# Hybrid attention and DeltaNet step: a modulation slab moved, column groups tied, late half norms, and weight splits taken off GpSimd

## Chip, cores and metric

The kernel runs on one core of a Trainium2 chip in one launch. The metric is device time in microseconds (us) of that core, as the median of several executions. One further execution was profiled, and the rows below come from it. Engine names are those of the profile: PE (TensorE matmul), PEld (its weight load), DVE (VectorE), ACT (ScalarE), POOL (GpSimd) and SP (SyncE, which issues most DMAs).

## What is computed (the reference, cut)

One step of a two layer model on 128 context tokens and 512 latent tokens, with width 1024. Layer 0 mixes tokens by attention, layer 1 by a gated delta rule; each layer has a squared ReLU MLP of width 4096. Each layer draws six modulation vectors from a conditioning vector, by one 1024 x 6144 matrix per layer.

```python
def modulation(cond, w_mod, b_mod):
    m = jax.nn.silu(cond) @ w_mod + b_mod
    return jnp.split(m[..., None, :], N_MOD, axis=-1)

def trunk_layer(x, mods, gain1, gain2, w1, w2, mixer):
    shift1, scale1, gate1, shift2, scale2, gate2 = mods
    mix, aux = mixer(rms_norm(x, gain1) * (1 + scale1) + shift1)
    x = x + gate1 * mix
    h = rms_norm(x, gain2) * (1 + scale2) + shift2
    x = x + gate2 * (jnp.square(jax.nn.relu(h @ w1)) @ w2)
    return x, aux
```

The attention mixer has 8 query heads over 2 key heads, with normalised and rotated queries and keys. The delta mixer has 8 heads, a short convolution, and a chunked recurrence in both directions. A final norm closes the step.

## The kernel before, in words

**Layout.** All 640 tokens are kept transposed as eight tiles of 128 features x 640 tokens. A dense product is made of 128 x 128 weight blocks against 320 tokens (one of two halves). Each operand is split into a high and a low part, and each product is three matmuls (`mm3`, L178). A weight column block of 1024 x 128 is loaded as a `raw` tile (L212, issued by SP), its high part is written by ACT and its low part, a subtraction, by DVE or by POOL (`pair`, L210, argument `eng`; the subtraction shows as L160). `raw` has 3 buffers, `wpair` (pinned weights, also used for slabs) has 6, `wx` has 10.

**Modulation slabs.** The 1024 x 6144 matrix of a layer is taken in three slabs of 2048 columns; slab (l, s) is slab s of layer l. `modulate` (L398) walks k over the eight blocks of 128 rows. Each k loads two 512 KB tiles of 1024 columns (or one of those and two of 512, `fetch_mixed`), and makes four matmuls of 32 output partitions x 512 columns (L408), one in each column group of the array (q = 0 to 3). In the trace one such matmul has two records. The result is transposed (L176) and becomes shifts, scales and gates (`modulation`, L415).

**Order of the work.** The program is traced in the order of generators that `weave` interleaves; the tile scheduler then sets each engine's order by its own estimate of when operands are ready, and the queues run in order. Stages of the profiled run, in us: start and slab (0,0) to 50; keys and values (`attn_kv`) with slab (0,1) 55 to 107; eight attention heads to 271; the output projection (`attn_w_out`) with slab (0,2) to 351; the first MLP to 800, with slab (1,0) from 376 to 428 and pre-split weights beside it; eight DeltaNet heads 810 to 1333, with slabs (1,1) and (1,2) from 1169 to 1325; the output projection `dn_w_out` to 1399; the second MLP to 1857; the final norm.

**What the change touches.** `attention` (L745) weaves slab (0,1) into `attn_kv`, with `raw` tiles and the PSUM tiles named `S`. `pinned` (L93) ties the work beside an MLP to its steps. `mod_norm(x, l, which, h, half)` (L316) makes one half of a norm: sums by matmuls named `nps` (L289), a short DVE chain `rsqrt` of tiny operations (`sso`, `rsy`, `rst` in the trace), then eight feature tiles. Both MLPs begin after `mod_norm(..., 1)` has been traced. The `dense` call of `dn_w_out` names `nc.gpsimd` for the low parts of the last five weight blocks, while the last DeltaNet head's output norm runs its `rsqrt` on DVE.

Of the kernel before, what the change touches and what calls it, by code (L numbers as in the profile page):

```python
# [23 lines left out]
HEADS = 8  # L24
# [53 lines left out]
def weave(*parts):  # L78
    live = [[0, n, i, g] for i, (g, n) in enumerate(parts)]
    while live:  # L80
        live.sort(key=lambda e: ((e[0] + 1) / e[1], e[2]))
        e = live[0]
        try:
            next(e[3])
            e[0] += 1
        except StopIteration:
            live.pop(0)
# [2 lines left out]
PINNED = tuple(getattr(mybir.EngineType, n) for n in ("PE", "DVE", "Activation"))  # L90


def pinned(tc, main, n, side, m):  # L93
    nc = tc.nc
    last = {}
    why = mybir.DependencyInfo(mybir.DependencyClass.NoSync, mybir.DependencyReason.DATA)
    traced = lambda i: nc.cur_bb.bb.instructions[i:]
    at = len(traced(0))
    done = step = 0
    for _ in main:  # L100
        step += 1
        for i in traced(at):
            if i.engine in PINNED:
                last[i.engine] = i.name
        at = len(traced(0))
        while done * n < step * m and next(side, True) is None:
            done += 1
            for i in traced(at):
                if i.engine in last:
                    tc.add_manual_dep(i, last[i.engine], why, reason="paced")  # L110
            at = len(traced(0))
    drain(side)


def drain(g):
    for _ in g:
        pass


class Model:  # L120
# [277 lines left out]
    def modulate(self, l, slab, fetch, alloc=None, early=False):  # L398
        nc = self.nc
        acc = alloc or (lambda: self.ps("mod", 1))  # L400
        ps = acc()[:, :512]
        get = lambda k: fetch(self.a["w_mod"][l, k * P : (k + 1) * P, slab * 2048 : (slab + 1) * 2048])
        ahead = get(0) if early else None
        for k in range(FT):
            views = ahead or get(k)
            ahead = get(k + 1) if early and k + 1 < FT else None
            for q in range(4):
                nc.tensor.matmul(  # L408
                    ps[32 * q : 32 * q + 32, :], self.cond[:, k, :], views[q],
                    start=k == 0, stop=k == FT - 1, tile_position=(0, 32 * q),  # L410
                )
            yield
        yield from self.modulation(l, slab, ps, acc)

# [330 lines left out]
    def attention(self, h, x):  # L745
        self.q, self.prob, self.att = {}, {}, []
        with self.psum("ps1") as self.pq:
            weave((self.attn_kv(h, x), 16), (self.modulate(0, 1, self.fetch_raw, lambda: self.ps("S", 2, 1024)), 9))
            weave((self.attn_scores(0), 8), (self.attn_proj(h, 1), 3))
            for hd in range(HEADS):  # L750
                parts = [(self.attn_values(hd), 6)]
                if hd + 1 < HEADS:
                    parts.append((self.attn_scores(hd + 1), 5))
                if hd + 2 < HEADS:
                    parts.append((self.attn_proj(h, hd + 2), 12))
                weave(*parts)

    def psum(self, name):
# [560 lines left out]
    def run(self):  # L1319
# [23 lines left out]
        with pool("mlp0") as self.ph, psum("ps3") as self.pq:  # L1343
            self.extra = 3
            x = self.reload(self.xd)
            h = self.new_h()
            nxt = []

            def mid():
                nxt[:] = self.prefetch(a["mlp_w1"][0], 0, FC)  # L1350
                self.mod_norm(x, 0, 1, h, 0)

            weave((self.modulate(0, 2, self.fetch_raw), 18),
                  (self.dense(a["attn_w_out"][0], 0, FC, self.att, self.residual(x, 0, 2), first=first, last=GROUP, mid=mid), 16))
            self.mod_norm(x, 0, 1, h, 1)
            h2 = self.new_h()
            nxt2 = []

            def mid2():
                w = a["dn_w_in"][0]  # L1360
                nxt2[:] = [self.pair(w, 0, kind * D) for kind in (1, 0, 2)]
                self.mod_norm(x, 1, 0, h2, 0)

            def beside():
                yield from self.modulate(1, 0, self.fetch_pairs, early=True)
                yield from self.presplit()

            pinned(tc, self.mlp(0, h, x, nxt, mid2), 128, beside(), 74)
            self.mod_norm(x, 1, 0, h2, 1)
            h = h2  # L1370
            xd = self.spill(x, nc.scalar)
# [5 lines left out]
        with pool("mlp1") as self.ph, psum("ps5") as self.pq:  # L1377
# [11 lines left out]

            done = len(self.first)  # L1390
            sink = self.residual(x, 1, 2)
            drain(self.dense(a["dn_w_out"][0], 0, FC[done:], acts, lambda o, half, ps: sink(o + done, half, ps), last=GROUP, mid=mid3, eng=nc.gpsimd))
            self.mod_norm(x, 1, 1, h, 1)
            fn = a["final_norm"]
            gain = self.wp.tile([P, D], F32, tag="wpair", bufs=self.NW, name="fgain")
            nc.scalar.dma_start(out=gain, in_=bass.AP(fn.tensor, fn.offset, [[0, P], [1, D]]))
# [1 line left out]
            def final(half):  # L1398
                cols = self.ps("nps", 2)
                if half == 0:  # L1400
                    blocks = (0, 1)
                    for i, b in enumerate(blocks):
                        self.rstd_cols(cols, i, [(0, P, 0, b * P)])
                else:
                    blocks = (2, 3, 4)
                    self.rstd_cols(cols, 0, [(0, P // 2, 0, 2 * P)])
                    self.rstd_cols(cols, 0, [(P // 2, P // 2, 1, 0)])
                    for i in (1, 2):
                        self.rstd_cols(cols, i, [(0, P, 1, (i + 2) * P - HALF)])
                r = self.finish_rstd(cols[:, : len(blocks)])  # L1410
                for i, b in enumerate(blocks):
                    y = self.wp.tile([P, D], F32, tag="wpair", bufs=self.NW, name=self.nm("y"))
                    for c in range(0, D, 512):
                        ps = self.dense_ps()
                        for j in range(4):
                            self.tr(ps[:, j * P : (j + 1) * P], x[c // P + j][:, b * P : (b + 1) * P])
                        out = y[:, c : c + 512]
                        if c == 0 or b == NBLK - 1:
                            self.stt(out, ps, r[:, i : i + 1], gain[:, c : c + 512], ALU.mult, ALU.mult)
                        else:  # L1420
                            self.act(out, ps, AF.Copy, scale=r[:, i : i + 1])
                            self.tt(out, out, gain[:, c : c + 512], ALU.mult, nc.gpsimd)
                        dst = self.o["y_prompt"][0] if b == 0 else self.o["y_sample"][0, (b - 1) * P : b * P, :]
                        (nc.sync if c else nc.scalar).dma_start(out=dst[:, c : c + 512], in_=out)

            drain(self.mlp(1, h, x, nxt3, lambda: final(0)))
            final(1)


# [39 lines left out]
```

## Time and profile before

| what | value |
|---|---|
| median of 3 runs | 1876.78 us (1871.9 to 1878.34) |
| the profiled execution | 1876.26 us, span of its instructions 1874.5 us |
| mean granted TensorE clock | 0.986 of full speed |
| PE busy / PEld / DVE / ACT / POOL | 95% / 88% / 53% / 40% / 16% of the span |
| bytes by DMA | 248.84 MB, 133 GB/s on average |

The span is the stretch from the first to the last instruction; the execution's own time is 1.8 us longer. Busy shares are averages over stages that differ: the rows further down are read stage by stage.

### The profile page before, as it was taken

The numbers are of one execution on the slowest core, as the hardware profiler recorded it, in microseconds if no ns is written. First come the engines' busy times: TensorE is split into PE (matmuls) and PEld (weight loads), VectorE is DVE, ScalarE is ACT, GpSimd is POOL, SyncE is SP. The second block draws the span as 40 slices with busy tenths as digits, with TensorE's granted clock in tenths as the row PEclk, the third lists the DMA queues.
The fourth block names the chain that finished last, engine by engine and source line by source line (L and its number), as shares of the span: only waits on it lengthen the run. The fifth ranks groups of instructions, "written<-read, shape, count | busy, mean of one in ns | idle before, by whom it ended". The sixth has DMA issues, their size and how long they took to land.

```text
span 1874.5 us, 31001 instructions
## 1 busy us (share of the span) xinstructions
PE 1786.5 (95%) x11971; PEld 1654.7 (88%) x11971; DVE 989.5 (53%) x2301; ACT 757.4 (40%) x1727; POOL 297.7 (16%) x390
## 2 busy tenths in 40 slices
PE   6998999999999999999899999999899999999997
PEld 3777877969999999999898998776699999999997
DVE  5546563724454544556788877443664334343332
ACT  3345552423342423436766565533343223131331
POOL 1143321400010010142021110110251000000012
PEclk8999999999999999999999999999999999999999
DMA  8641136365576676625432333654721222222211
GB/s 322 203 149 35 35 125 205 93 207 178 177 221 194 208 221 189 190 78 175 122 104 83 105 101 112 183 162 139 235 78 57 70 79 74 73 80 71 76 46 57
DMA packets 286761, 248.84 MB, mean 133 GB/s; under 512 B 44591, under 2 KB 246726, under 8 KB 286614
## 3 DMA queue, kind: packets, MB, share of 16 engines
q1 hardware_dynamic: 266768, 207.85, 36.9%
q0 software_dynamic: 9136, 32.18, 4.8%
q10 hardware_dynamic: 10710, 6.83, 1.2%
q8 instruction: 94, 1.54, 0.4%
q14 instruction: 53, 0.43, 0.1%
HBM read 199.00 MB, written 45.20 MB: 130 GB/s over the span
## 4 chain that ended last, share of the span: by engine, by line
PE 75%; DVE 12%; DMA 6%; ACT 2%; issue 2%; POOL 1%; SPq 1%; ACTq 0%; POOLq 0%; DVEq 0%
PE dense L173 33%; PE pd L173 29%; PE scan L173 3%; PE big L173 3%; DVE ptmp L160 2%; PE pd L408 2%; PE mod L408 1%; DMA wide<-gd 1%; DMA raw<-in_w_mod 1%; PE big L176 1%; DVE ptri L1066 1%; DVE cv L166 1%; DMA wm<-in_w_mod 1%; PE S L173 1%; DVE pv L160 1%
## 5 line engine op out<-in xcount | busy, mean ns | idle before, releaser
L173 PE MATMUL pd<-h,w 128*128 128x320 f32 x2016 | 350.6, 319 | 7.8 <-ACT cv L163 3.3
L173 PE MATMUL dense<-a,wx 128*128 128x320 f32 x2238 | 339.7, 311 | 2.4 <-ACT wx L163 1.6
L173 PEld LDWEIGHTS dense<-a,wx 128*128 128x128 f32 x2238 | 332.8, 189 | 5.2 <-ACT wx L163 2.5
L173 PEld LDWEIGHTS pd<-h,w 128*128 128x128 f32 x2016 | 299.0, 189 | 35.1 <-issue 21.8
L163 ACT ACTIVATE wx<-raw 128x1024 fp32r<-128x1024 f32 x132 | 139.8, 1059 | 360.9 <-PE dense L173 217.1
L173 PE MATMUL dense<-h,wx 128*128 128x320 f32 x1776 | 266.8, 309 | 0.0
L173 PEld LDWEIGHTS dense<-h,wx 128*128 128x128 f32 x1776 | 261.6, 188 | 5.9 <-issue 5.0
L160 DVE TENSOR_TENSOR wx<-raw,wx 128x1024 fp32r<-128x1024 f32 x127 | 159.1, 1255 | 156.7 <-ACT wx L163 156.7
L173 PE MATMUL pd<-a,wx 128*128 128x320 f32 x1284 | 194.3, 309 | 0.0
L173 PEld LDWEIGHTS pd<-a,wx 128*128 128x128 f32 x1284 | 189.8, 188 | 0.0
L166 DVE SCALAR_TENSOR_TENSOR x<-dense,c,x 128x192 f32<-128x192 f32 (+2 forms) x147 | 59.7, 434 | 176.0 <-PE dense L173 175.9
L173 PE MATMUL pd<-h,wx 128*128 128x320 f32 x1008 | 151.9, 309 | 0.0
L173 PEld LDWEIGHTS pd<-h,wx 128*128 128x128 f32 x1008 | 148.7, 188 | 1.7 <-DVE a L160 1.7
L160 POOL TENSOR_TENSOR x<-x,half 128x320 f32<-128x320 f32 x48 | 54.1, 1128 | 527.1 <-ACT half L163 526.4
L163 ACT ACTIVATE a<-half 128x320 fp32r<-128x320 f32 x128 | 59.9, 471 | 112.6 <-DVE half L166 112.6
L160 DVE TENSOR_TENSOR a<-half,a 128x320 fp32r<-128x320 f32 x128 | 62.7, 492 | 65.1 <-ACT a L163 65.1
L166 DVE SCALAR_TENSOR_TENSOR x<-pd,c,x 128x128 f32<-128x128 f32 (+2 forms) x87 | 35.8, 440 | 104.9 <-PE pd L173 104.9
L908 POOL DMA_DIRECT2D wd<-w x58 | 30.9, 534 | 369.3 <-ACT w L163 293.2
L166 DVE SCALAR_TENSOR_TENSOR cv<-cv,c,cv 128x644 f32<-128x644 f32 x84 | 78.5, 935 | 17.1 <-ACT cv L163 16.0
L163 ACT ACTIVATE half<-x 128x320 f32<-128x320 f32 x56 | 25.9, 467 | 101.9 <-DVE x L166 101.9
L173 PE MATMUL big<-wide,a 128*128 128x128 f32 x480 | 63.5, 278 | 1.2 <-DMA wide<-td 0.9
L173 PEld LDWEIGHTS big<-wide,a 128*128 128x128 f32 x480 | 58.0, 191 | 7.1 <-ACT a L163 3.1
(289 smaller groups left out, 2486.1 us busy)
## 6 DMA issues: line engine op xcount, KB each, us to landing
raw<-in_mlp_w SPq DMA_DIRECT2D x128, 512.0 KB
wd<-w POOLq DMA_DIRECT2D x58, 512.0 KB, 4.5
w<-wd SPq DMA_DIRECT2D x58, 512.0 KB
raw<-in_w_mod SPq DMA_DIRECT2D x48, 512.0 KB
wm<-in_w_mod SPq DMA_DIRECT2D x32, 512.0 KB
rawp<-in_dn_w_in SPq DMA_DIRECT2D x58, 256.0 KB
a<-in_w_mod SPq DMA_DIRECT2D x32, 256.0 KB
raw<-in_attn_w_in SPq DMA_DIRECT2D x12, 512.0 KB
```

Of the source, the lines that this page charges most:

```text
L160: (eng or self.nc.vector).tensor_tensor(out=out, in0=in0, in1=in1, op=op)
L163: self.nc.scalar.activation(out=out, in_=in_, func=func, **kw)
L166: self.nc.vector.scalar_tensor_tensor(out=out, in0=in0, scalar=s, in1=in1, op0=op0, op1=op1)
L173: self.nc.tensor.matmul(out, l, r, start=first, stop=last)
L176: self.nc.tensor.transpose(out, in_, self.ident[:n, :n])
L408: nc.tensor.matmul(ps[32 * q : 32 * q + 32, :], self.cond[:, k, :], views[q], start=k == 0, stop=k == FT - 1, tile_position=(0, 32 * q),)
L908: self.nc.gpsimd.dma_start(out=d[z], in_=pair[z].bitcast(F32).rearrange("p k c -> p (k c)"))
L1066: nc.vector.tensor_reduce(out=t[:, BASE * i : BASE * i + i], in_=o, axis=AX.X, op=ALU.add)
```

## The change

It has five parts. **A**: slab (0,1) leaves `attn_kv` and runs beside `attn_values` of heads 6 and 7, with weight tiles from `wpair`, a PSUM tile of the dense pool, and the next k's tiles fetched one k ahead. **B**: the four matmuls of one k are given in the order q = 3, 2, 1, 0, and each is tied behind the one before it by a dependency that only orders. **C**: in both MLPs the second half of the norm ahead is traced after the first step of the MLP. **D**: beside the first MLP the slab's generator yields twice for each step, and the count of side steps goes from 74 to 83. **E**: the last five `dn_w_out` blocks make their low parts on DVE.

```diff
+ORDER = mybir.DependencyInfo(mybir.DependencyClass.NoSync, mybir.DependencyReason.DATA)
+def late(g, f):
+    yield next(g)
+    f()
+    yield from g
...
-            for q in range(4):
+            prev = None
+            for q in (3, 2, 1, 0):
                 nc.tensor.matmul(
                     ps[32 * q : 32 * q + 32, :], self.cond[:, k, :], views[q],
                     start=k == 0, stop=k == FT - 1, tile_position=(0, 32 * q),
                 )
+                i = nc.cur_bb.bb.instructions[-1]
+                assert i.engine == PINNED[0]
+                if prev is not None:
+                    self.tc.add_manual_dep(i, prev, ORDER, reason="side by side")
+                prev = i.name
...
-            weave((self.attn_kv(h, x), 16), (self.modulate(0, 1, self.fetch_raw, lambda: self.ps("S", 2, 1024)), 9))
+            drain(self.attn_kv(h, x))
+            wm = self.modulate(0, 1, self.fetch_pairs, self.dense_ps, True)
...
                 if hd + 2 < HEADS:
                     parts.append((self.attn_proj(h, hd + 2), 12))
+                else:
+                    parts.append((islice(wm, 5 if hd == HEADS - 2 else 4), 6))
...
-            self.mod_norm(x, 0, 1, h, 1)
...
-                yield from self.modulate(1, 0, self.fetch_pairs, early=True)
+                for _ in self.modulate(1, 0, self.fetch_pairs, early=True):
+                    yield
+                    yield
                 yield from self.presplit()
-            pinned(tc, self.mlp(0, h, x, nxt, mid2), 128, beside(), 74)
+            main = late(self.mlp(0, h, x, nxt, mid2), lambda: self.mod_norm(x, 0, 1, h, 1))
+            pinned(tc, main, 128, beside(), 83)
...
-            drain(self.dense(a["dn_w_out"][0], 0, FC[done:], acts, lambda o, half, ps: sink(o + done, half, ps), last=GROUP, mid=mid3, eng=nc.gpsimd))
-            self.mod_norm(x, 1, 1, h, 1)
+            drain(self.dense(a["dn_w_out"][0], 0, FC[done:], acts, lambda o, half, ps: sink(o + done, half, ps), last=GROUP, mid=mid3))
...
-            drain(self.mlp(1, h, x, nxt3, lambda: final(0)))
+            drain(late(self.mlp(1, h, x, nxt3, lambda: final(0)), lambda: self.mod_norm(x, 1, 1, h, 1)))
```

How the order of instructions moves is shown at three places. In the changed kernel the helpers' lines are 8 to 9 higher (L181 is the old L173, L184 the old L176, L417 the old L408, L168 the old L160).

The first place is PE in `attn_kv`. Before, pieces of slab (0,1) (`S<-raw`) stand between the products of keys (`pd`, 128 x 256).

```order
L173 MATMUL pd_624<-w_296,h_341 128x256
L408 MATMUL S_487<-raw_488,c_100 32x512 x2
L173 MATMUL pd_624<-w_297,h_341 128x256
L173 MATMUL pd_624<-w_296,h_342 128x256
L173 MATMUL pd_624<-w_300,h_343 128x256
L173 MATMUL pd_624<-w_301,h_343 128x256
L173 MATMUL pd_624<-w_300,h_344 128x256
L173 MATMUL pd_624<-w_300,h_345 128x256
L173 MATMUL pd_624<-w_301,h_345 128x256
```

In the changed kernel no slab stands there. Its k-steps are now found in heads 6 and 7, between scores (`S<-key`), transposed probabilities (`pt`) and value products (`pd<-pv,val`):

```order
L184 MATMUL pt_2633<-c_85,x_2581 128x128
L181 MATMUL S_2655<-key_723,x_2493 128x320
L417 MATMUL pd_2642<-wm_2645,c_100 32x512 x2
L417 MATMUL pd_2642<-wm_2643,c_100 32x512 x2
L181 MATMUL S_2655<-key_724,x_2493 128x320
L181 MATMUL S_2655<-key_723,x_2494 128x320
L184 MATMUL pt_2670<-c_85,x_2465 128x128
L184 MATMUL pt_2670<-c_85,x_2527 128x128
L184 MATMUL pt_2670<-c_85,x_2554 128x128
L184 MATMUL pt_2670<-c_85,x_2581 128x128
L181 MATMUL pd_2632<-pv_2638,val_983 128x512
L181 MATMUL pd_2632<-pv_2639,val_983 128x512
```

Each k is one run of four, with the tiles of the second load (`wm_2645`) ahead of those of the first. All eight k stand between there and the end of head 7.

The second place is PE in the DeltaNet heads, where slab (1,1) begins (`pd<-raw` and `pd<-a` with `c_100`; `scan` and `big` are the recurrence, `pd<-h,w` a dense product). Before, its matmuls came one or two at a time:

```order
L173 MATMUL pd_12754<-h_3738,w_12738 128x320
L173 MATMUL pd_12754<-h_3740,w_12737 128x320
L173 MATMUL pd_12754<-h_3741,w_12737 128x320
L173 MATMUL pd_12754<-h_3740,w_12738 128x320
L408 MATMUL pd_12827<-raw_12828,c_100 32x512
L173 MATMUL scan_12711<-yb_12697,wide_10867 128x128 x2
L408 MATMUL pd_12827<-raw_12828,c_100 32x512
L173 MATMUL pd_12754<-h_3742,w_12737 128x320
```

Now it begins later, with k whole, and behind a row of recurrence steps without dense products between them:

```order
L181 MATMUL scan_12968<-blk_12909,a_11475 128x128
L181 MATMUL scan_12968<-blk_12910,a_11475 128x128
L181 MATMUL scan_12968<-yb_12913,wide_11465 128x128 x2
L181 MATMUL scan_13006<-blk_12973,x_11069 128x128
L181 MATMUL scan_13006<-blk_12975,x_11069 128x128
L181 MATMUL scan_13006<-blk_12973,x_11244 128x128
L181 MATMUL scan_13006<-blk_12975,x_11244 128x128
L181 MATMUL big_12919<-wide_12775,a_12917 128x128 x2
L417 MATMUL pd_12827<-a_12832,c_100 32x512
L417 MATMUL pd_12827<-a_12830,c_100 32x512
L417 MATMUL pd_12827<-raw_12828,c_100 32x512 x2
L181 MATMUL pd_12899<-h_3667,w_12737 128x320
```

The matmul that waits for all four tiles stands in the queue ahead of the dense products of `pd_12899`.

The third place is DVE in the last DeltaNet head, where `a<-h,a` are low parts of activations and the chain of `sso`, `rst` and `rsy` is the output norm. Before:

```order
L160 TENSOR_TENSOR a_13953<-scan_14299,a_13953 128x128
L160 TENSOR_TENSOR a_14307<-h_14304,a_14306 128x640
L170 TENSOR_SCALAR sso_14339<-sso_14339 128x5
L166 SCALAR_TENSOR_TENSOR sso_14339<-ssc_12744,sso_14339 128x5
L170 TENSOR_SCALAR rsy_14348<-sso_14339 128x5
L160 TENSOR_TENSOR rst_14349<-rsy_14348 128x5
L166 SCALAR_TENSOR_TENSOR rst_14349<-rst_14349,sso_14339 128x5
L166 SCALAR_TENSOR_TENSOR rsy_14348<-rst_14349,rsy_14348 128x5
```

Now the low parts of `dn_w_out` (`wx<-raw,wx`, 128 x 1024) stand in the chain:

```order
L168 TENSOR_TENSOR w_14336<-raw_14333,w_14335 128x1024
L168 TENSOR_TENSOR a_14307<-h_14304,a_14306 128x640
L168 TENSOR_TENSOR wx_14590<-raw_14587,wx_14589 128x1024
L178 TENSOR_SCALAR sso_14339<-sso_14339 128x5
L174 SCALAR_TENSOR_TENSOR sso_14339<-ssc_12744,sso_14339 128x5
L178 TENSOR_SCALAR rsy_14348<-sso_14339 128x5
L168 TENSOR_TENSOR rst_14349<-rsy_14348 128x5
L174 SCALAR_TENSOR_TENSOR rst_14349<-rst_14349,sso_14339 128x5
L168 TENSOR_TENSOR wx_14596<-raw_14593,wx_14595 128x1024
L174 SCALAR_TENSOR_TENSOR rsy_14348<-rst_14349,rsy_14348 128x5
L168 TENSOR_TENSOR rst_14349<-rsy_14348 128x5
L174 SCALAR_TENSOR_TENSOR rst_14349<-rst_14349,sso_14339 128x5
```

Three of the five come ahead of the product `a_13953<-a_13953,rsy_14348` that ends the chain, one right behind it, and the last behind `a_14367`.

## Rows read from the trace of the kernel before

**Rows 1.** The page: span; the chain by engine; GB/s in 40 slices of the span.

```profile
span 1874.5 us, 31001 instructions
...
PE 75%; DVE 12%; DMA 6%; ACT 2%; issue 2%; POOL 1%; SPq 1%; ACTq 0%; POOLq 0%; DVEq 0%
...
GB/s 322 203 149 35 35 125 205 93 207 178 177 221 194 208 221 189 190 78 175 122 104 83 105 101 112 183 162 139 235 78 57 70 79 74 73 80 71 76 46 57
```

**Rows 2.** Two stretches: us; PE, PEld, DVE, ACT, POOL busy; PEclk; DMA share; GB/s.

```profile
1165.00:1330.00 165.00, 159.12 (x990) 115.72 (x989) 77.39 (x269) 69.02 (x234) 21.25 (x20) 1.00 0.57 180
...
1325.00:1350.00 25.00, 16.49 (x105) 15.15 (x103) 21.45 (x31) 12.51 (x26) 12.36 (x5) 0.89 0.70 212
```

**Rows 3.** The slab matmuls' line: durations in ns, and what its engine awaited.

```profile
L408 PE MATMUL pd<-raw,c x64: 592/593/617, 1169.6 to 1324.6; 128*32 128x512 f32 x64
...
  DMA raw<-in_w_mod: 11.8, 13
```

**Rows 4.** PE timeline, keys and values (start, us, engine, what, records, wait).

```profile
60.29 1.05 PE L408 MATMUL S<-raw,c 128*32 128x512 f32 x4 [0.61 <-DMA raw<-in_w_mod]
...
105.22 1.05 PE L408 MATMUL S<-raw,c 128*32 128x512 f32 x4 [1.50 <-DMA raw<-in_w_mod]
...
107.39 2.00 PE L173 MATMUL S<-key,x 128*128 128x320 f32 x12
...
111.14 3.49 PE L173 MATMUL pd<-h,w 128*128 128x320 f32 x22 [1.17 <-POOL w L160]
```

**Rows 5.** PE timeline, `attn_w_out` with slab (0,2), and entry of MLP 0.

```profile
270.84 1.90 PE L408 MATMUL mod<-raw,c 128*32 128x512 f32 x10
...
278.77 1.05 PE L408 MATMUL mod<-raw,c 128*32 128x512 f32 x4 [1.33 <-DMA raw<-in_w_mod]
...
279.75 3.79 PE L173 MATMUL dense<-a,w 128*128 128x320 f32 x24
...
283.47 1.06 PE L408 MATMUL mod<-raw,c 128*32 128x512 f32 x8
...
288.18 1.61 PE L408 MATMUL mod<-raw,c 128*32 128x512 f32 x8
...
320.43 1.05 PE L408 MATMUL mod<-raw,c 128*32 128x512 f32 x4
...
353.02 0.38 PE L289 MATMUL nps<-c,x 128*128 128x1 f32 x2 [2.44 <-POOL x L160]
```

**Rows 6.** PE timeline, first MLP with slab (1,0).

```profile
376.38 1.05 PE L408 MATMUL mod<-wm,c 128*32 128x512 f32 x4 [0.53 <-DMA wm<-in_w_mod]
...
419.57 1.07 PE L408 MATMUL mod<-wm,c 128*32 128x512 f32 x8
```

**Rows 7.** PE timeline, first matmul of slab (1,1) and last of slab (1,2).

```profile
1169.56 1.04 PE L408 MATMUL pd<-raw,c 128*32 128x512 f32 x2
...
1324.20 0.62 PE L408 MATMUL pd<-a,c 128*32 128x512 f32 x2
```

**Rows 8.** PE timeline, the last DeltaNet head's end.

```profile
1347.82 1.33 PE L176 MATMUL big<-c,a 128*128 128x128 f32 x5 [6.97 <-DVE a L160]
...
1348.80 3.89 PE L173 MATMUL scan<-a,w 128*128 128x320 f32 x17
```

**Rows 9.** DVE timeline, same place.

```profile
1330.16 1.22 DVE L160 TENSOR_TENSOR w<-raw,w 128x1024 fp32r<-128x1024 f32 x1
...
1332.23 0.82 DVE L160 TENSOR_TENSOR a<-h,a 128x640 fp32r<-128x640 f32 x1
...
1333.41 2.57 DVE L160 TENSOR_TENSOR a<-h,a 128x640 fp32r<-128x640 f32 x1 [0.16 <-ACT a L163]
...
1338.29 2.33 DVE L166 SCALAR_TENSOR_TENSOR sso<-ssc,sso 128x5 f32<-128x5 f32 x1
...
1345.54 0.17 DVE L166 SCALAR_TENSOR_TENSOR rsy<-rst,rsy 128x5 f32<-128x5 f32 x1
```

**Rows 10.** POOL timeline, same place.

```profile
1332.88 10.02 POOL L160 TENSOR_TENSOR wx<-raw,wx 128x1024 fp32r<-128x1024 f32 x4 [42.63 <-ACT wx L163]
```

More of the change, by code (lines that the diff above doesn't have):

```diff
@@ L95, in pinned @@
     last = {}
-    why = mybir.DependencyInfo(mybir.DependencyClass.NoSync, mybir.DependencyReason.DATA)
     traced = lambda i: nc.cur_bb.bb.instructions[i:]
@@ L109, in pinned @@
                 if i.engine in last:
-                    tc.add_manual_dep(i, last[i.engine], why, reason="paced")
+                    tc.add_manual_dep(i, last[i.engine], ORDER, reason="paced")
             at = len(traced(0))
```

## The prediction

> **What bounds the kernel now.** I read the page first: in the chain that ended last PE has 75% and DVE 12%, in a span of 1874.5 us [rows 1]. So time comes out where PE work disappears from a stretch that PE fills, or where PE stands still. Next I read PE's busy time by stretch: in 1165 to 1330 it works 159.1 of 165 us, so the DeltaNet rounds with slabs are nearly full; in 1325 to 1350 it works only 16.5 of 25, at a granted clock of 0.89 [rows 2]. Third came the line of the slab matmuls and the PE timeline around them. The reader is to see one pattern: a group of slab matmuls occupies PE for about the same time whether it has one matmul (two records, 1.04 us [rows 7]), two (four records, 1.05 [rows 4]) or all four of a k (eight records, 1.07 [rows 6]). The next instruction begins about 0.98 us after such a group's start: so a k costs 1.0 us whole, 2.0 in halves and nearly 4 singly. Last, I read what ends PE's idle time: tiles of slabs at the loads of `raw` (11.8 us in 13 waits [rows 3], some of it at the start), POOL's sums ahead of an MLP, and DVE at the end of the last DeltaNet head.
>
> I sum against the profiled execution, 1876.26 us (its span and 1.8 around it), which is 0.5 us under the median. A difference of 0.3% (5.6 us) is about what a measurement of this kernel can tell from no change.
>
> **Part A, out of `attn_kv`.** Between 60.29 and 105.22 slab (0,1) has sixteen groups of two matmuls; each holds PE for 0.98, together 15.7 us. Waits for tiles ahead of four of them (0.61 at the first, 1.50 at the last) make 2.8. Behind the last group, which ends near 106.2, stand ACT's copy and four transposes up to the first scores at 107.39: 1.2 [rows 4]. Sum −19.7. It is all on PE's path, as the scores stand behind it in the queue. Bounds: −15.7, if only the matmuls come out because rotated keys are late next (key products now end earlier, and POOL, SP and DVE have the same work for them), and −20.9, if the following wait of 1.17 for POOL's low part [rows 4] goes too. I take −20: POOL has no more to do before it than it had, but it also has less time.
>
> **Part A, into heads 6 and 7.** Eight whole k at 1.0 and the transposes give +8.4. They lie between score and value matmuls, where PE is in order and mostly busy. The tiles are ten of sixteen behind the first three k, 5.2 MB in some 17 us, or 310 GB/s; the best slice of the page, 47 us long, moved 322 [rows 1]. So I add 1.5 of waiting, with bounds 0 (groups fill PE's small gaps) and 5 (the tiles arrive at 240 GB/s, close to the other full slices, and the 17 us become 22). **+9.9.**
>
> **Slab (0,2) beside `attn_w_out`.** The ten rows of its matmuls from 270.84 to 320.43 sum to 12.5 us; eight whole k take 8: −4.5. The wait of 1.33 for a tile goes, as k 0 is no longer cut: −1.3. But a k now wants both its tiles at its first matmul, and three `raw` buffers hold one and a half k. The group at 283.47 ended and freed its tiles near 284.5; the group at 288.18 lasted 1.61 in place of 1.07, so its second tile came near 288.7: 4.2 us from release to landing [rows 5]. In the new queue 57, 21, 21, 21, 18 and 6 dense matmuls stand between k 0 and k 6, at 0.155 each (24 from 279.75 to 283.47 [rows 5]). Behind k 1 that fills 3.3, 3.3, 3.3, 2.8 and 0.9 us of 4.2: waits of 0.9 three times, 1.4 and 3.3, together 7.4. **+1.6**, bounds −5.8 (tiles always there) and +5 (the load of the next dense block, queued behind them, is late as well).
>
> **Slab (1,0) in the first MLP.** Thirteen groups from 376.38 to 419.57, ten of them halves, become eight: −4.9. Two waits for tiles like the one at 376.38 (together 1.2) go, since the steps are now twice as far apart [rows 6]. The MLP fills PE, so **−6**, bounds −4 to −6.5.
>
> **Slabs (1,1) and (1,2) in DeltaNet.** The two have 64 matmuls, half of them on `raw` [rows 3], in 39 groups that hold PE for 38.2 us; the first is that at 1169.56, the last that at 1324.20 [rows 7]. Sixteen whole k take 16: −22.2 of PE work. PE is 96% busy there [rows 2], so most of it should be time. But the slab also filled PE while the recurrence waited for DVE and ACT, and the new order has runs of `scan` steps with no dense product between. The chain cannot get shorter; idle time of 5.9 us in this stretch shows that it already shows through. Bounds −22 (all realized) and −8 (each round a little over 2 us shorter); I take **−16**, nearer to the full stretch's row than to a chain limit that no row shows.
>
> **Part E, the last head.** The transposes at 1347.82 waited 6.97 us for DVE [rows 8]. DVE's operations there take 2.57 in place of 0.8 and about 2.3 in place of 0.17 [rows 9], exactly while POOL makes four low parts in 10.02 us [rows 10]. The Trainium skill says that GpSimd's interfaces to SBUF are shared with VectorE, with contention for DVE instructions with two SBUF inputs (GPSIMD Engine Reference, Specifications). The trace agrees in the first of these rows, but shows it for tiny operations with one input too. Without POOL the chain costs 0.8 for the low part, twelve small operations at 0.2, and 0.8 for the product: 4.0, plus three low parts of `wx` that stand among them, at the 1.22 of such a part on DVE [rows 9]: 7.7. From 1333.41 that is 1341.1 in place of 1347.7, **−6.6**. The 17 matmuls behind took 3.89 in place of 2.6 at a lower granted clock, which a shorter stop spares: −1.3; the fifth low part ahead of DVE's last step costs 0.4 back. **−7.5**; bounds −9, and −3 if a low part waits in DVE's queue for its tile, with the chain behind it.
>
> **Part C.** At 353.02 PE waited 2.44 us for POOL's sum [rows 5]; the entry of the second MLP repeats that. Now 24 dense matmuls (3.7 us) stand ahead of the sums, more than the wait that they cover: the sums come up to 1.3 later and the half's norm with them, and the dense products of that half need it. Bounds for each are −2.4 (all covered) and +1.3 (the norm's delay is paid in full); I take −0.7, near the middle: **−1.5** together. Part D only spaces the pre-split work, which the MLP's full PE hides; uncovered, its DVE and ACT work would show as waits of `pd<-h,wx` for operands: 0 to +2.
>
> **Start, slab (0,0).** Its end hangs on its last tile, tied or not: 0.
>
> **Sum.** −20 +9.9 +1.6 −6 −16 −7.5 −1.5 = −39.5, which gives 1836.8; I say **1837**.
>
> **Rivals.** *Tiles at the heads* (chance 0.13). Ten `wm` tiles, then `raw` tiles and eight reloads of x stand in SP's queue one behind the other. If heads 6 and 7 wait 5 us and the block after them 5, it ends near 1844. For it: 310 GB/s against 322. Against: three k are loaded ahead.
>
> *The recurrence is the bound* (0.22). Then −8 replaces −16: 1845. For it: the runs of `scan`. Against: waits of PE there sum to only 5.9 us.
>
> *Whole k stop the queue* (0.04, slower). Forty-eight k now wait for the last of four operands with the whole of PE behind them. From 0.82 us of added wait for each (39.5 / 48) the gain is gone, and at 1.0 it ends near 1885. Slab (0,2) shows how: 7.4 us for eight. Against: slabs (1,0) and (0,1) are fetched one k ahead, and those in DeltaNet have several us between k's. The Trainium skill has the rule: matmuls start and end strictly in program order (TensorE: Matmul & The Clock Gate, What overlaps and what doesn't). It agrees with the idle time ahead of 278.77, where dense products stood behind a late tile.
>
> *Larger gain* (0.09). Full realization in DeltaNet and no waits in `attn_w_out`: about 1825.
>
> **Numbers.** The forecast's own case, 1830 to 1843, has 0.52. With the rivals next to it, 1821 to 1855 holds 8 in 10 and a little more. Faster by over 0.3%: 0.93; same 0.03; slower 0.04.
>
> **What would show it.** First scores near 87 and heads ending near 261; sixteen groups of eight records from 1169 on, and PE's idle time in these rounds under 12 us; waits for `raw` in `attn_w_out` of about 7 us; transposes of the last head some 7 us after the head's last low part begins, not 14, with DVE's small operations at 0.17 to 0.2. Wrong would be: PE waiting for key rotation near 87, for `wm` in heads 6 and 7, or for `scan` operands between 1165 and 1310 by more than the 6 us that I leave for it.

## Result and profile after

The changed kernel takes 1849.72 us (median of 4 runs, 1846.62 to 1852.04) against 1875.6 for the kernel before (4 runs). The ratio is 0.9867 with a 95% interval of 0.9843 to 0.9891: 1.3% faster. I had forecast 1837, so two thirds of the 39.5 us came. The profiled execution is the fastest of the four, 1846.62, with a span of 1844.8; the one before was near its median, so the two spans differ by 29.7 us where the medians differ by 25.9. The page begins with the span; the chain that ended last is not shown, as it covers little more than a third of the span.

```profile
span 1844.8 us, 30993 instructions
```

Six places of PE's timeline cut both spans in the same way. First the changed kernel: first scores, first matmul of slab (0,2), last product of `attn_w_out`, first sum of the second layer's norm, first product of `dn_w_out` (`pd<-a,w`), and the first of its products that stand behind the last head's transposes (`big<-a,w`).

```profile
92.02 2.02 PE L181 MATMUL S<-key,x 128*128 128x320 f32 x12
...
257.44 1.06 PE L417 MATMUL mod<-raw,c 128*32 128x512 f32 x8
...
339.56 7.19 PE L181 MATMUL pd<-a,wx 128*128 128x320 f32 x48
...
798.14 0.28 PE L297 MATMUL nps<-c,x 128*128 128x1 f32 x2
...
1306.78 0.41 PE L181 MATMUL pd<-a,w 128*128 128x320 f32 x1
...
1322.68 6.31 PE L181 MATMUL big<-a,w 128*128 128x320 f32 x42
```

The same of the kernel before, where [rows 4] and [rows 5] have the first two:

```profile
343.37 7.21 PE L173 MATMUL pd<-a,wx 128*128 128x320 f32 x48
...
808.33 0.28 PE L289 MATMUL nps<-c,x 128*128 128x1 f32 x2
...
1328.53 1.63 PE L173 MATMUL pd<-a,w 128*128 128x320 f32 x8 [0.28 <-ACT x L163]
...
1352.53 3.69 PE L173 MATMUL big<-a,w 128*128 128x320 f32 x24
```

| stretch, us | before | after | difference | forecast |
|---|---|---|---|---|
| start to first scores | 107.4 | 92.0 | −15.4 | −20 |
| heads | 163.4 | 165.4 | +2.0 | +9.9 |
| `attn_w_out` with slab (0,2), to the end of its last product | 79.7 | 89.3 | +9.6 | +1.6 |
| first MLP, with its entry | 457.7 | 451.4 | −6.4 | −6.7 |
| DeltaNet, to the first product of `dn_w_out` | 520.2 | 508.6 | −11.6 | −16 |
| the last head's end | 24.0 | 15.9 | −8.1 | −7.5 |
| the rest | 522.0 | 522.1 | +0.1 | −0.7 |
| sum | 1874.5 | 1844.8 | −29.7 | −39.4 |

Four of the terms are off by 4 us or more. The rows behind them follow, from PE's timeline of the changed kernel where nothing else is said. In `attn_kv` a new wait stands where the slab was, for DVE's scaled keys:

```profile
69.67 0.69 PE L184 MATMUL S<-c,a 128*128 128x128 f32 x2 [2.94 <-DVE a L178]
```

Beside `attn_w_out` each k from the third on waits for its tiles, six waits of together 8.2 us (four are shown). Behind them PE waits 3.43 us for POOL's sums, and then matmuls take 0.30 us in place of 0.155:

```profile
272.28 1.06 PE L417 MATMUL mod<-raw,c 128*32 128x512 f32 x8 [0.79 <-DMA raw<-in_w_mod]
...
287.81 1.06 PE L417 MATMUL mod<-raw,c 128*32 128x512 f32 x8 [1.31 <-DMA raw<-in_w_mod]
...
293.32 1.07 PE L417 MATMUL mod<-raw,c 128*32 128x512 f32 x8 [3.37 <-DMA raw<-in_w_mod]
295.98 0.90 PE L181 MATMUL dense<-a,wx 128*128 128x320 f32 x2 [1.59 <-ACT wx L171]
...
309.44 1.06 PE L417 MATMUL mod<-raw,c 128*32 128x512 f32 x8 [1.07 <-DMA raw<-in_w_mod]
...
322.79 0.59 PE L297 MATMUL nps<-c,x 128*128 128x1 f32 x2 [3.43 <-POOL x L168]
323.24 3.02 PE L181 MATMUL dense<-a,wx 128*128 128x320 f32 x10
```

The same two places before. The wait for a `wx` is not new, but the sums followed without a wait there, and the ten matmuls took 1.71 us:

```profile
306.16 0.56 PE L173 MATMUL dense<-a,wx 128*128 128x320 f32 x2 [1.60 <-ACT wx L163]
...
330.60 1.71 PE L173 MATMUL dense<-a,wx 128*128 128x320 f32 x10
```

POOL's sum waits for ACT's square, that for DVE's update of x, and this stands in DVE's queue behind the low part of a weight of the first MLP, whose load is late:

```profile
318.27 1.06 ACT L171 ACTIVATE w<-raw 128x1024 fp32r<-128x1024 f32 x1 [1.76 <-DMA raw<-in_mlp_w]
```

In DeltaNet PE stands still 15 us ahead of the first k of slab (1,1), and its next matmuls run slowly (10 in 2.34 us). The k itself follows without a wait:

```profile
1158.86 1.12 PE L181 MATMUL pd<-h,w 128*128 128x320 f32 x6
1165.91 1.33 PE L184 MATMUL big<-c,a 128*128 128x128 f32 x5 [5.93 <-POOL a L168]
1167.03 2.34 PE L181 MATMUL big<-wide,a 128*128 128x128 f32 x10
...
1180.79 0.62 PE L417 MATMUL pd<-a,c 128*32 128x512 f32 x2
```

PE's waits in these rounds, as totals, times and the longest one; first before (1160 to 1328), then after (1148 to 1306):

```profile
PE big L176 <- POOL a L160: 2.7, 5, 0.8
PE scan L173 <- DVE blk L166: 0.8, 2, 0.5
```

```profile
PE big L184 <- POOL a L168: 10.4, 6, 5.9
PE scan L181 <- DVE blk L174: 3.9, 4, 1.9
```

At the entry of the first MLP the wait is 2.08 in place of 2.44 [rows 5], and ends with ACT's square of the last tile. ACT shows why: it waits for the load of a weight before it splits it (`wx`), and the square stands behind that split.

```profile
352.46 0.59 PE L297 MATMUL nps<-c,half 128*128 128x1 f32 x2 [2.08 <-ACT half L171]
```

```profile
350.99 1.06 ACT L171 ACTIVATE wx<-raw 128x1024 fp32r<-128x1024 f32 x1 [1.83 <-DMA raw<-in_mlp_w]
351.95 0.45 ACT L171 ACTIVATE half<-x 128x320 f32<-128x320 f32 x1
```

In the last head DVE's tiny operations take 0.16 to 0.17 (2.33 before [rows 9]), with the `wx` parts among them; the transposes wait 0.62 us:

```profile
1314.27 0.16 DVE L178 TENSOR_SCALAR sso<-sso 128x5 f32<-128x5 f32 x1
...
1317.74 1.22 DVE L168 TENSOR_TENSOR wx<-raw,wx 128x1024 fp32r<-128x1024 f32 x1 [0.48 <-ACT wx L171]
...
1319.27 0.83 DVE L168 TENSOR_TENSOR a<-a,rsy 128x640 f32<-128x640 f32 x1
```

```profile
1320.15 0.77 PE L184 MATMUL big<-c,a 128*128 128x128 f32 x5 [0.62 <-DVE a L168]
```

### The profile page after: what moved, and what is told of

It is laid out like the page before. It is cut to its first block, busy times and chain, and to the rows that moved or that the text cites. A ratio compares the mean times of both kernels' runs of the same rounds, so it can differ in the third digit from the quotient of the medians.

```text
span 1844.8 us, 30993 instructions
## 1 busy us (share of the span) xinstructions
PE 1741.5 (94%) x11971; PEld 1650.0 (89%) x11971; DVE 986.6 (53%) x2306; ACT 759.1 (41%) x1727; POOL 284.0 (15%) x385
## 5 line engine op out<-in xcount | busy, mean ns | idle before, releaser
L181 PE MATMUL pd<-h,w 128*128 128x320 f32 x2016 | 347.5, 318 | 7.4 <-ACT cv L171 3.6
L181 PE MATMUL dense<-a,wx 128*128 128x320 f32 x2238 | 341.8, 312 | 2.0 <-ACT wx L171 1.6
L181 PEld LDWEIGHTS dense<-a,wx 128*128 128x128 f32 x2238 | 334.5, 190 | 5.8 <-ACT wx L171 2.5
L181 PEld LDWEIGHTS pd<-h,w 128*128 128x128 f32 x2016 | 298.9, 189 | 20.1 <-issue 7.5
L181 PE MATMUL dense<-h,wx 128*128 128x320 f32 x1776 | 265.3, 309 | 0.0
L181 PEld LDWEIGHTS dense<-h,wx 128*128 128x128 f32 x1776 | 261.5, 188 | 2.5 <-issue 2.5
L168 DVE TENSOR_TENSOR wx<-raw,wx 128x1024 fp32r<-128x1024 f32 x132 | 165.9, 1259 | 161.5 <-ACT wx L171 161.5
L181 PE MATMUL pd<-a,wx 128*128 128x320 f32 x1284 | 194.3, 309 | 0.0
L181 PEld LDWEIGHTS pd<-a,wx 128*128 128x128 f32 x1284 | 189.6, 188 | 0.8 <-issue 0.8
L181 PE MATMUL pd<-h,wx 128*128 128x320 f32 x1008 | 151.7, 309 | 0.0
L181 PEld LDWEIGHTS pd<-h,wx 128*128 128x128 f32 x1008 | 148.7, 188 | 0.8 <-DVE a L168 0.8
L168 POOL TENSOR_TENSOR x<-x,half 128x320 f32<-128x320 f32 x48 | 53.3, 1112 | 567.6 <-ACT half L171 510.4
L168 DVE TENSOR_TENSOR a<-half,a 128x320 fp32r<-128x320 f32 x128 | 62.9, 492 | 66.3 <-ACT a L171 66.0
L181 PE MATMUL big<-wide,a 128*128 128x128 f32 x480 | 65.3, 284 | 1.2 <-DMA wide<-td 0.9
L181 PEld LDWEIGHTS big<-wide,a 128*128 128x128 f32 x480 | 60.2, 197 | 4.5 <-issue 1.6
```

The source lines that it names most:

```text
L168: (eng or self.nc.vector).tensor_tensor(out=out, in0=in0, in1=in1, op=op)
L181: self.nc.tensor.matmul(out, l, r, start=first, stop=last)
```

## Experiments

Each kernel is the changed one with one edit, or with several where it is said (6 and 7). The experiments ran in three sets (1 to 4, 5 to 8, 9 to 11). "Before" ran in each set on the same chip and took 1873 to 1875 us; the changed kernel did not, so across sets the ratios to "before" are compared. Its own is 0.9867 (0.9843 to 0.9891), and a total whose ratio lies within 0.003 to 0.004 of that is not clear of noise by itself. In edits 1 and 4 `tie` is a new argument of `modulate`; where it is false the order is q = 0 to 3 and nothing ties. Two theories stood at first. Theory 1: a tied k with three `raw` buffers makes PE, and all that stands behind in the queues, wait for loads. Theory 2: in DeltaNet the recurrence, not PE, sets half of the rounds.

**1. Slab (0,2) untied.**

```diff
-            weave((self.modulate(0, 2, self.fetch_raw), 18),
+            weave((self.modulate(0, 2, self.fetch_raw, tie=False), 18),
```

> The changed kernel, but the four matmuls of a k of slab (0,2), beside attn_w_out, are left untied and in the order q = 0 to 3; the other slabs stay tied. In the changed kernel the stage from the first matmul of slab (0,2) to the first product of the MLP lasts 89.2 us (79.6 before the change) and PE waits 8.2 us for raw tiles there. Theory 1 (a whole k wants both tiles at once, with three buffers of raw and 4.2 us from release to landing, and everything behind it in the queues is late): the stage falls to 78 to 82 us, waits for raw under 3, the total 7 to 11 us below the changed kernel, near 1841. Rival (the loads of x and of the weights, crowded together since the heads end earlier, hold the tiles up whatever the order): the stage stays at 86 to 90 us and the total within 3 us of the changed kernel.

Measured: 1844.42 us, ratio to before 0.9833 (0.9804 to 0.9862). The stage, as the table measures it, is 81.3 us (89.3), no wait for `raw` is left, and the span is 7.7 us shorter. Theory 1 holds for the stage. The median fell by 5.3, less than expected and not clear of noise.

**2. Four `raw` buffers, nine `wx`.**

```diff
-    NX, NH, NA, NW, NRAW, NWX = 12, 16, 16, 6, 3, 10
+    NX, NH, NA, NW, NRAW, NWX = 12, 16, 16, 6, 4, 9
```

> The changed kernel with four raw buffers in place of three (and nine wx in place of ten, for the room). Theory 1: two whole k fit, the tiles of a k are asked for one k earlier, PE's waits for raw beside attn_w_out fall from 8.2 us to under 2, and the stage of 89.2 us to 79 to 83; the total 6 to 10 us below the changed kernel. Rival (crowded loads, so the DMA rate decides): waits stay over 5 us and the stage over 86.

Measured: 1855.99, where 6 to 10 us less than in the changed kernel was expected; the ratio of 0.9894 (0.9865 to 0.9923) does not tell it from the changed kernel. But the stage is 77.1 us, and one wait of 2.2 us for `raw` is left. The loss came later: DeltaNet with its entry is 14 us longer than in the changed kernel and the part behind the last head 8. There, from 1320 on, PE waits for POOL's sums, behind the last groups of five blocks, which want ten `wx`:

```profile
PE nps L297 <- POOL x L168: 5.2, 3, 4.0
```

So theory 1 holds for the stage. That nine `wx` cost the rest fits experiment 7, which has ten and neither loss, but no run changes that number alone; part of the loss is clock (0.95 in the DeltaNet rounds with slabs, 0.97 in the changed kernel).

**3. DeltaNet without its slabs.**

```diff
-                yield from self.modulate(1, slab, self.fetch_mixed, self.dense_ps, True)
+                nc.vector.memset(self.mods[1][:, slab * 16 : slab * 16 + 16, :], 0.5)
+                if slab == 2:
+                    nc.vector.memset(self.gains[1][1], 0.5)
+                yield
```

> The changed kernel without slabs (1,1) and (1,2): their loads, matmuls and transposes are left out, and a constant stands for the modulation of the second layer that they would give. It takes 16 us of matmuls and 0.9 us of transposes from PE in the DeltaNet rounds. Theory 2 (the recurrence's chain through DVE, ACT and POOL sets a good part of these rounds, so PE work taken out turns into waits): the total falls by 4 to 9 us only, and PE's waits between the last full round and the last head's output rise from 18 us to over 26. Rival (PE is the bound, and only the place of the whole k costs): the total falls by 14 to 18 us and waits stay near 18 us.

Measured: 1826.45, 23 us less. From the second layer's first norm to the last head's end it took 502.8 us against 524.5 in the changed kernel: −21.8 for 16.9 us of PE work. PE's waits between the last full round and the last head's output came to 14 us, not to over 26. Theory 2 falls: PE is the bound, and more than the work itself went. What went with it shows in the wait for POOL before the transposes, longest 2.9 us now and not 5.9, and in a granted clock of 1.00 in place of 0.97 (from 1148 on):

```profile
PE big L184 <- POOL a L168: 7.4, 6, 2.9
1148.00:1299.00 151.00, 135.58 (x987) 126.98 (x987) 96.65 (x304) 75.97 (x251) 21.30 (x20) 1.00 0.35 107
```

```profile
1148.00:1299.00 151.00, 133.09 (x964) 113.49 (x962) 78.41 (x272) 63.00 (x222) 21.18 (x20) 0.97 0.55 175
```

**4. DeltaNet's slabs untied.**

```diff
-                yield from self.modulate(1, slab, self.fetch_mixed, self.dense_ps, True)
+                yield from self.modulate(1, slab, self.fetch_mixed, self.dense_ps, True, False)
```

> The changed kernel, but the matmuls of slabs (1,1) and (1,2) in DeltaNet untied and in the order q = 0 to 3; the other slabs stay tied. Theory 2 (22 us of PE work were worth 10.8 us, since the rest turned into waits for the recurrence): these rounds get 9 to 12 us longer, PE's waits there fall from 18 to about 6 us, the total rises to about 1860. Rival (the tied k wait for their late tiles and so cost the other half): they get under 6 us longer, total below 1856.

Measured: 1859.15, and the stretch of the rounds is 520.4 us (520.2 before, 508.6 changed). The tie gave the whole difference, 11.7 us. These are the numbers that theory 2 expected, though experiment 3 speaks against it; the trace offers another cause for the lost half. The waits for POOL are 3.0 us here, and 20 dense matmuls (behind two slab matmuls) fill PE where it stood 5.9 us:

```profile
1160.90 1.58 PE L181 MATMUL pd<-h,w 128*128 128x320 f32 x9
1163.01 1.88 PE L181 MATMUL pd<-h,w 128*128 128x320 f32 x11 [0.53 <-ACT x L171]
```

In the changed kernel's queue these 20 (`pd_12899`) stand behind the tied first k, whose `a` tiles SP asks for only at 1175.49, and with it behind the transposes that wait for POOL at 1165.91. That is theory 3, which the next run tests.

**5. The first k of slab (1,1) untied.** `loose` names the k's that are not tied.

```diff
-                yield from self.modulate(1, slab, self.fetch_mixed, self.dense_ps, True)
+                yield from self.modulate(1, slab, self.fetch_mixed, self.dense_ps, True, (0,) if slab == 1 else ())
```

> The changed kernel with the first k of slab (1,1) alone untied and in the order q = 0 to 3. Theory 3 (the tied first k, which waits for its late tiles, stands in PE's queue ahead of 20 dense matmuls; these no longer fill the wait for POOL before the transposes, PE stands 5.9 us there, and its clock falls): the wait for POOL falls to under 2 us, the granted clock of that stretch is 1.00 again, and the stretch from the second layer's first norm to the last head's output, 508.6 us in the changed kernel, falls to 500 to 504. Rival (the wait is the chain's own and only moves to the next place): the stretch stays over 507 us.

Measured: 1841.96, ratio 0.9836 (0.9821 to 0.9851). The wait for POOL is 5.1 us in all, its longest 2.0. The stretch is 506.9 us in this profile, between what the two sides expected. PE's idle time in it fell from 34.9 to 28.3 us, but the clock stayed at 0.97, where theory 3 had expected 1.00; the same rounds take 501.2 at a clock of 1.00 in the next experiment.

```profile
PE big L184 <- POOL a L168: 5.1, 5, 2.0
1137.00:1317.00 180.00, 167.61 (x1178) 141.87 (x1177) 103.07 (x333) 81.82 (x263) 21.43 (x20) 0.97 0.59 184
```

**6. Both repairs.** Edits 1 and 5 together.

> The changed kernel with both repairs: slab (0,2) untied beside attn_w_out, and the first k of slab (1,1) untied. If the two causes are independent, as theories 1 and 3 have it, the gains add: some 8 us and some 6 us, a span near 1831 and a median near 1837. Rival (one gain is given back behind the other, by a wait that comes later): a median of 1843 or more.

Measured: 1832.86, ratio 0.9784 (0.977 to 0.9799). The span of 1829.5 is within 2 us of the one expected, the median is 4 us better. Against experiment 1 the ratios differ by 0.0049, or 9 us, for the untied first k. Of these, idle time is 6.9 (34.8 to 27.9 in the stretch); the rest came with the clock. Theory 3 holds for the wait; why the clock came back here and not in experiment 5 is open.

```profile
1132.00:1307.00 175.00, 163.85 (x1179) 138.49 (x1178) 102.64 (x333) 81.47 (x262) 21.45 (x20) 1.00 0.60 189
```

**7. Four `raw`, ten `wx`, the first k untied; slab (0,2) stays tied.** Edit 5, and the room for the fourth buffer from the pre-split:

```diff
-    NX, NH, NA, NW, NRAW, NWX = 12, 16, 16, 6, 3, 10
+    NX, NH, NA, NW, NRAW, NWX = 12, 16, 16, 6, 4, 10
...
-        return self.scr("rawp", 3, [P, FT // 2, P])
+        return self.scr("rawp", 2, [P, FT // 2, P])
...
-        raws = [load(*x) for x in steps[:2]]
+        raws = [load(*x) for x in steps[:1]]
...
-            if n + 2 < len(steps):
-                raws.append(load(*steps[n + 2]))
+            if n + 1 < len(steps):
+                raws.append(load(*steps[n + 1]))
```

> The changed kernel with four raw buffers, ten wx as before (the room comes from the pre-split's pieces, two in place of three), and the first k of slab (1,1) untied; slab (0,2) stays tied. Theory 1: the stage of slab (0,2) is 77 us as with four raw before, and the waits at the entries of the two second norms that nine wx cost do not come: the total 3 to 5 us below the kernel with both repairs, near 1833. Rival (the fourth raw itself, by earlier loads, slows DeltaNet and the second MLP): the stretches behind the first MLP stay 8 us or more longer than in the changed kernel, total over 1842.

Measured: 1815.82 (1813.43 to 1817.15), ratio 0.9691 (0.9677 to 0.9706): 3.1% below the kernel before, and far below what I expected. The stage of slab (0,2) is 72.7 us, at a clock of 1.00 (85.6 and 0.96 in experiment 5). A further 3.9 and 3.4 us against experiment 6 lie in the two MLPs: the waits at their entries are gone. At the first one the sums follow one another without a wait, and the dense products behind run at 0.155:

```profile
332.71 0.28 PE L297 MATMUL nps<-c,x 128*128 128x1 f32 x2
332.85 0.36 PE L297 MATMUL nps<-c,half 128*128 128x1 f32 x2
...
337.64 4.50 PE L181 MATMUL dense<-h,w 128*128 128x320 f32 x29
```

So the lack of one buffer made three of the waits: beside slab (0,2) and at both entries. DeltaNet took 3.9 us of the gain back. The pre-split's lost piece is the one other thing that differs from experiment 5. Whether a fourth buffer would have helped the kernel before was not tried.

**8. Part A undone.**

```diff
-            drain(self.attn_kv(h, x))
-            wm = self.modulate(0, 1, self.fetch_pairs, self.dense_ps, True)
+            weave((self.attn_kv(h, x), 16), (self.modulate(0, 1, self.fetch_raw, lambda: self.ps("S", 2, 1024)), 9))
...
-                else:
-                    parts.append((islice(wm, 5 if hd == HEADS - 2 else 4), 6))
```

> The changed kernel without part A: slab (0,1) stands beside attn_kv again with raw tiles and the S tiles, but tied. Theory 4 (in heads 6 and 7 the slab's groups fill waits of value products for DVE, so eight groups cost 2 us there and not 8; in attn_kv they and their tiles' waits are paid in full): first scores come 12 to 18 us later than in the changed kernel, near 106, the heads are 2 to 3 us shorter, the total 10 to 15 us longer, near 1862. Rival (tied groups are cheap in attn_kv too, and the gain was mostly from tying): under 6 us longer.

Measured: 1860.88, ratio 0.9942 (0.9921 to 0.9962), first scores at 108.3; the heads take 166.3 us without the slab in them (165.4 with it), and did not get shorter, against theory 4. But their clock is 0.96 in this run and 1.00 in the changed kernel, so it cannot tell filled waits from a faster clock. The tied k wait 11.2 us for `raw` in `attn_kv`, the last one 4.18:

```profile
104.83 1.94 PE L417 MATMUL S<-raw,c 128*32 128x512 f32 x8 [4.18 <-DMA raw<-in_w_mod]
```

So tying alone would have given nothing there. The `attn_w_out` stage is 82.8 us; most of its k stand 23 to 25 products apart, where part A left 57, 21 and 6. So of the 9.6 us the tie makes some 3 by itself, and the rest comes from tie and move together.

**9. Part C undone.** `mod_norm(..., 1)` stands ahead of each MLP again.

```diff
+            self.mod_norm(x, 0, 1, h, 1)
...
-            main = late(self.mlp(0, h, x, nxt, mid2), lambda: self.mod_norm(x, 0, 1, h, 1))
+            main = self.mlp(0, h, x, nxt, mid2)
...
+            self.mod_norm(x, 1, 1, h, 1)
...
-            drain(late(self.mlp(1, h, x, nxt3, lambda: final(0)), lambda: self.mod_norm(x, 1, 1, h, 1)))
+            drain(self.mlp(1, h, x, nxt3, lambda: final(0)))
```

> The changed kernel without part C: both second halves of the norms stand ahead of the MLPs again. By the prediction's term (0.7 us for each) the total rises by 1.5 us. By the trace of the changed kernel (PE still waits 2.1 and 2.3 us at the two entries, for ACT's square now and not for POOL's sum) it is within 1.5 us of the changed kernel, and the waits of 2.4 us for POOL come back in place of these. Rival (the dense products of the second half now wait for the late norm): it falls by 2 us or more.

Measured: 1850.6, no difference in the median (ratio 0.9877, 0.9852 to 0.9903). Waits of 2.5 us for POOL stand at both entries again.

**10. Part E undone.** `eng=nc.gpsimd` is back in the `dense` call of `dn_w_out`.

> The changed kernel without part E: POOL makes the low parts of the last five dn_w_out blocks again. By the ledger of the two traces (the last head's end, from its first product of dn_w_out to the last sum over it, took 24.0 us before and 15.9 after) the total rises by 7 to 9 us and tiny DVE operations of 2.3 us return. Rival (that end is shorter because the slabs' last matmuls left it): it rises by under 4 us.

Measured: 1858.5, 8.8 more, ratio 0.9912 (0.9886 to 0.9939); the last head's end is 24.4 us (15.9), and a tiny operation takes 2.28:

```profile
1316.18 2.28 DVE L174 SCALAR_TENSOR_TENSOR rsy<-rst,rsy 128x5 f32<-128x5 f32 x1
```

**11. Part D undone.** One slab step for each side step, and 74 of them.

> The changed kernel without part D: a slab step for each side step again, and 74 of them. By the prediction (spacing only removes two waits for tiles of slab (1,0), together 1.2 us, and moves pre-split work that the MLP hides) the total rises by 0 to 3 us. Rival (tied k, twice as dense, wait for tiles at each k, as beside attn_w_out): waits for wm tiles of over 4 us appear between 374 and 420 and the total rises by 4 us or more.

Measured: 1850.91, within noise of the changed kernel; the first MLP with its slab takes 451.0 us (451.4), and no wait for `wm` appears. The spacing is worth nothing that could be measured.

## Why the prediction was right, and where it was short

The time fell inside the wide range and outside my own case, 1830 to 1843. Two of the terms below were off by 8 us each, one too high and one too low, and that they cancel is luck.

**Out of `attn_kv`** (−15.4 for −20): 0.3 us short of the lower bound that I named, −15.7, and for much the reason named with it. All slab work and its waits went, and keys are late next: 2.94 us for DVE's scaling, at 69.67 and not near 87, and 1.1 for values.

**Heads** (+2.0 for +9.9): over-priced. No wait for a `wm` tile came, for which I had 1.5. In the rows below (first the heads before, then after; PE's busy time stands behind the length) PE's idle time falls from 13.6 to 11.1 us, and its busy time rises by 4.5 only, not by 8.4, while the clock rises from 0.98 to 1.00. I had the idle time in my bounds only, and the clock not at all. That the slab's work raised the clock is not shown: experiment 8 has the heads without it, at 0.96.

```profile
107.40:270.80 163.40, 149.81 (x937) 133.94 (x934) 105.06 (x285) 91.10 (x196) 64.08 (x61) 0.98 0.22 65
```

```profile
92.00:257.40 165.40, 154.30 (x1004) 132.18 (x1002) 103.68 (x288) 91.50 (x196) 56.04 (x58) 1.00 0.28 88
```

**Slab (0,2)** (+9.6 for +1.6): the step that failed most. Its waits for tiles were right one by one (8.2 for 7.4; the wait of the last k, 1.07, was not in the sum). What it left out is what comes behind them. The load of the next dense block is late, as I had it only in the bound of +5; it reaches PE as 3.4 us for POOL's sums, while the wait for `wx` is as long as before. The clock, which I had not at all, makes the matmuls from there to 332 take 3.9 us more than before, about what the whole k save. Theory 1's two tests, by the tie and by a fourth buffer, gave 8 and 12 us. With four buffers and ten `wx` (experiment 7) the stage is 7.0 us shorter than before, a little beyond my bound of −5.8 for tiles that are always there.

**Slab (1,0) and part C** (−6.4 for −6.7): right in sum. The two waits for `wm` go because a k is whole, not because its steps stand further apart (experiment 11). Part C by itself gave nothing measurable, for a reason that I had not seen: the last square stands behind a weight split that waits for a `raw` tile (experiment 7).

**DeltaNet** (−11.6 for −16): PE's work was the measure, as forecast, not the recurrence: that rival lost with experiment 3, though its −8 was a little nearer. PE's busy time in the stretch fell by 23.6 us (497.3 to 473.7), but its idle time grew by 12.0, and in the rounds with slabs it was 18 us where I had written under 12. What was missing is mostly one hole. The first k stands late in the queue and 20 dense matmuls behind it, so these could not fill the wait of the transposes ahead of it. This is near the rival on whole k's that stop the queue, which showed here and at the six waits of slab (0,2), and hardly at the other k's. The Trainium skill has matmuls start and end strictly in program order (TensorE: Matmul & The Clock Gate, What overlaps and what doesn't). The trace agrees: none of the 20 passed the transposes in their 5.93 us. Untying this one k gave back 6.6 to 6.9 us of idle time, and 6 to 9 us of the total. Some 5 us of added idle time stay (27.9 in experiment 6 for 22.9 before): so much of the recurrence does show through, and I had allowed 6 of the 22.

**Part E** (−8.1 for −7.5): right by mechanism and size; experiment 10 gives 8.8.

Still open: why the scheduler left uneven distances between the k's of slab (0,2) once part A was there, how much of the heads is clock, and what sets it. None was tried alone.

## What to carry to other kernels

Tying operations into one run saves PE time only where all their operands are there together. Count the buffers for whole steps, not for tiles, before tying: here one more buffer of 512 KB, with its room taken from a stage that had some to spare, was worth 26 us (experiment 7 against 5), as much as the whole change. An in-order queue makes one late operand the wait of everything behind it, so look first at what a scheduler placed behind the first step of a stream. Work put beside a chain of waits can cost a fourth of its own time (heads 6 and 7, 2.0 us of 8.4, though part of that is clock); work taken from ahead of a chain can turn into the wait for it (2.94 us for the keys).

## What was not expected of the hardware

A stop of PE can cost more than its length, but the same stop does not always do so. In the changed kernel ten matmuls of 320 columns behind the wait of 3.43 us in `attn_w_out` took 3.02 us, at the lower of the two levels (1.2 GHz), and the granted clock of the stage was 0.91 on average. In experiment 5, with the same program there, they took 1.71, at 2.4 GHz, behind a wait of 2.84; the clock of the stage was 0.96, and it was 3.7 us shorter though PE's idle time was the same (13.7 and 13.6 us).

```profile
257.00:347.00 90.00, 76.38 (x477) 66.88 (x476) 34.28 (x70) 25.59 (x44) 20.45 (x23) 0.91 0.58 180
```

```profile
323.20 0.38 PE L297 MATMUL nps<-c,x 128*128 128x1 f32 x2 [2.84 <-POOL x L168]
323.44 1.71 PE L181 MATMUL dense<-a,wx 128*128 128x320 f32 x10
...
257.00:343.50 86.50, 72.79 (x478) 62.70 (x479) 34.34 (x71) 25.61 (x44) 20.35 (x23) 0.96 0.60 188
```

Tiny DVE operations of 0.17 us last up to 2.4 while POOL makes the low parts of weights. Before, this holds for operations with one input too, which the rows ahead of the prediction do not show:

```profile
1340.65 2.28 DVE L170 TENSOR_SCALAR rsy<-sso 128x5 int32<-128x5 int32 x1
```

In experiment 10 three of the twelve in the chain took 2.2 to 2.3, and each of the three ends within 0.03 us of the end of a low part on POOL. For the one at 1316.18, shown there, this is POOL's row:

```profile
1316.10 2.34 POOL L168 TENSOR_TENSOR wx<-raw,wx 128x1024 fp32r<-128x1024 f32 x1 [0.58 <-ACT wx L171]
```

An engine off the critical path so held up operations with hardly any data, and that was worth 8 us in one place.
